# Hybrid gated-DeltaNet / mLSTM layer on one core: small-product banks kept by count, a decay chain on every second step, and a shorter last norm

## The chip, the cores and the metric

One Trainium2 chip, one of its cores. The metric is the device time of one execution in microseconds (us); lower is better. Three runs of the kernel before gave 1633.6, 1635.83 and 1637.04 us.

## The reference

One decoder layer, batch 1, 256 positions, width 2048, all in float32:

```python
shift, scale, gate = split(silu(c) @ w_ada + b_ada)
h = rms_norm(x, norm_pre_w) * (1 + scale) + shift
proj = h @ w_in                       # 12 segments, 24656 columns
o_a = gated_delta_rule(conv(q), conv(k), conv(v), decay, beta)    # 32 value heads, chunks of 64
y_a = (rms_norm(o_a) * silu(z)) @ w_proj_gdn
h_b = mlstm_chunkwise(conv(q), conv(k), v, i, f)                  # 8 heads
y_b = (sigmoid(o) * rms_norm(h_b) * silu(z)) @ w_proj_mlstm
out = (sigmoid(g_a) * y_a + sigmoid(g_b) * y_b) @ w_out
x + gate * rms_norm(out, norm_post_w)
```

The decay of the delta rule and the input and forget gates of the mLSTM come from 80 of the columns of `h @ w_in` (a softplus, exponentials and running sums along the sequence).

## The kernel before

The large products run on TensorE in a split form: each float32 weight tile `raw` is cast on ScalarE (ACT) to a reduced-precision `whi` (L168), the rest `wlo = raw - whi` is formed on VectorE (DVE) or, early on, GpSimd (POOL) (L169), and `mm3` (L217) sums three products. Four `whi` and four `wlo` buffers stand between these engines and TensorE, so a tile can be prepared up to four steps ahead.

The order of the work is fixed when the program is written, by two objects. `Stream` (L62) walks a list of weight units. Each unit has one or two uses, and one use is a **step**: 12 products of 512 columns or 24 products of 256 columns. After a use, the unit's `after` function may run, then `side.step()` is called once, then the next tile is prepared. `Side` (L30) holds generators of small work; a step lets each of them go on to its next `yield`. `wait(n)` yields n times. Each engine runs what it was given in that order, and never takes a later instruction first.

In order, the program goes through: the conditioning vector and the first gate columns (14 groups of 512 columns, added up over five blocks of rows by `add_start_groups`, L381); in the last block the 80 decay and gate columns come first (`add_ab`, product `pab`) and their chain `gates` (L433) runs as side work beside the 14 groups; then eight periods of delta-rule heads (`gdn_period`, L869), four rounds of mLSTM heads, the two output projections (`py`), and the last product `w_out` (`pw`).

In the last block of the 14 groups, every second step ends a group. Its `after` (L400) adds the two product banks to the sum so far on DVE (L405, twice), takes a sigmoid or silu of 1024 columns on ACT (L410), and stores it.

Within a period, side work prepares two head pairs (`gdn_stage1`, L604), inverts the chunk triangles (`base_inverse`, L670) and solves for the outputs (`gdn_stage2`, L725). The last of `gdn_stage2` transposes the outputs of two pairs into a bank each (`pt`, L848) and copies each bank out on ACT (`oT`, L850).

TensorE's result memory is used as four banks for the large products (`jtile`, pool `pj`) and four for the small ones (`gtile`, pool `pg`). The kernel keeps its own book of the small banks: `gtile` assumes that the four are given in turn, and `banks(n)` yields until the next n in turn were freed in an earlier step.

The last function, `finish` (L1168), closes the norm of one half of the rows: it sums four partial sums of squares, takes the power on POOL, and scales and adds the residual for four blocks of 512 columns, three on DVE (L1182) and one on ACT and POOL (L1179, L1180), each then stored.

Of the kernel before, what the change touches and what calls it, by code (L numbers as in the profile page):

```python
# [19 lines left out]
EPS = 1e-6  # L20
# [96 lines left out]
def hybrid_layer_kernel(  # L117
# [33 lines left out]
    pg = None  # L151
# [35 lines left out]
        split_w(raw[:, h * 1024:h * 1024 + n], hi[:, 0:n], lo[:, 0:n])  # L187
        return hi, lo

    freed = [-1] * 4  # L190
    slots = [0, {}]

    def gtile(nm, held=False):
        i = slots[0] % 4
        slots[0] += 1
        t = pg.tile([P, 512], F32, name=nm, tag="g")
        freed[i] = 1 << 30 if held else side.t + 1
        slots[1][id(t)] = i, t
        return t

    def gfree(t):
        freed[slots[1].pop(id(t))[0]] = side.t

    def banks(n):

        while any(freed[(slots[0] + j) % 4] >= side.t for j in range(n)):
            yield

    def jtile(nm):
        return pj.tile([P, 512], F32, name=nm, tag="pj")  # L210

    def pow_(o, i, e):
        G.tensor_tensor(o, i, e, op=ALU.pow)

    def mm3(ps, lhi, llo, rhi, rlo, start, stop):
        for i, (l, r) in enumerate(((lhi, rhi), (lhi, rlo), (llo, rhi))):
            T.matmul(ps, l, r, start=start and i == 0, stop=stop and i == 2, skip_group_check=True)  # L217

    side = Side()
    bp = x0 = y0 = None  # L220
# [52 lines left out]
    late_c = {}  # L273
# [64 lines left out]
    def ada_units():  # L338

        adders = []  # L340
        for k in range(KC):
            for pt in range(2):
                def prep(h, raw, k=k, pt=pt):
                    V.scalar_tensor_tensor(raw, raw, 1.0, csil, op0=ALU.mult, op1=ALU.mult,
                                           accum_out=ad[:, pt * KC + k:pt * KC + k + 1])
                    if 4 <= 2 * k + pt < 8:
                        j = 2 * (2 * k + pt)
                        if j > 8:
                            x_turn(j)
                        if j < 14:  # L350
                            x_scale(j + 2)
                    h_chunks(k - 1)
                    if pt == 1:
                        due.append(k)
                        if k == 0:
                            h_chunks(0)
                            x_chunks(6, 10)
                        elif k == KC - 1:
                            share[1] = 0.0
                    return ()  # L360
                adders.append(lambda i=2 * k + pt, prep=prep:
                              stream.add(w_ada[i], prep, None, 1, load=(load_ada, "ada", ADA_BUFS)))
        return adders

    br = ExitStack()

    def branches_open():

        nonlocal bp, pg, x0, y0
        side.drain()  # L370
        st.close()
        pcs.close()
        pg = ctx.enter_context(tc.tile_pool(name="pg", bufs=4, space=PSUM))
        bp = br.enter_context(tc.tile_pool(name="bp", bufs=2))

        x0 = bp.tile([P, 8, P], F32, name="x0", tag="x0", bufs=1)
        y0 = bp.tile([64, 8, 64], F32, name="y0", tag="y0", bufs=1)
        G.memset(x0, 0.0)
        G.memset(y0, 0.0)
# [53 lines left out]
    def gates(ps):  # L433
# [6 lines left out]
            return work[:, len(used) - 1]  # L440
        xb, ab, e, u, l, r = (t_(n) for n in ("xb", "ab", "e", "u", "l", "r"))
        V.tensor_scalar(xb, ps[:, 0:S], late_c["abb"][:, 0:1], None, op0=ALU.add)
        yield
        A.activation(ab, xb, AF.Abs)
        A.activation(e, ab, AF.Exp, scale=-1.0)
        na = gp.tile([32, 1], F32, name="na")
        A.activation(na, late_c["alog"], AF.Exp)
        yield
        V.tensor_scalar(u, e, 1.0, None, op0=ALU.add)
        yield  # L450
        A.activation(l, u, AF.Ln)
        A.activation(r, l, AF.Exp, scale=-1.0)
        yield
        V.tensor_scalar(u, u, -1.0, None, op0=ALU.add)
        V.tensor_tensor(e, e, u, op=ALU.subtract)
        V.tensor_tensor(e, e, r, op=ALU.mult)
# [13 lines left out]
                                 op0=ALU.mult, op1=ALU.add)  # L470
        V.tensor_tensor_scan(bf[96:104], on_[96:104], mn[96:104], 0.0, op0=ALU.mult, op1=ALU.add)
        SP.dma_start(bm[64:72], bf[96:104])
        yield
        A.activation(gt[32:64], mn[32:64], AF.Exp)
        yield
        V.tensor_tensor(gt[64:72], xb[64:72], bm[64:72], op=ALU.subtract)
        V.tensor_tensor_scan(mm_[64:72], zz[64:72], gt[64:72], 0.0, op0=ALU.add, op1=ALU.max)
        V.tensor_tensor(bm[64:72], bm[64:72], mm_[64:72], op=ALU.add)
        yield
# [4 lines left out]
        yield  # L484
        yield
        tp = jtile("tp")
        for b in range(2):
            T.transpose(tp[:, b * P:(b + 1) * P], gt[:, b * P:(b + 1) * P], ident)
            T.transpose(tp[:, S + b * P: S + (b + 1) * P], g2[:, b * P:(b + 1) * P], ident)
# [4 lines left out]
    def add_ab():  # L494
        st_ = {}

        def use(h, hi, lo):
            if h == 0:
                st_["ps"] = jtile("pab")
            for j in range(8):  # L500
                k = h * 8 + j
                h_chunks(k)
                mm3(st_["ps"][:, 0:S], hi[:, j * P:(j + 1) * P], lo[:, j * P:(j + 1) * P], h_hi[:, k], h_lo[:, k],
                    k == 0, k == KC - 1)
        stream.add(w_ab, prep_w, use, after=lambda: side.add(gates(st_["ps"])))
# [70 lines left out]
    o_dr = dr.tile([32, P, S], F32, name="o_dr")  # L576
    hb_dr = dr.tile([KC, P, S], F32, name="hb_dr")

    def wait(n):
        for _ in range(n):  # L580
            yield
# [22 lines left out]
    def gdn_stage1(p, ps, res):  # L604
# [48 lines left out]
        for blk, ps_, n, c0 in ((0, psa, 256, 0), (1, psb, 128, 512)):  # L653
            yield
            side.debt += 1.45 if blk == 0 else 1.0
            for h in range(2):
                V.scalar_tensor_tensor(au[:, h, c0:c0 + 2 * n].rearrange("p (a b) -> p a b", a=2),
                                       ps_[:, 0:2 * n].rearrange("p (a b) -> p a b", a=2), cj[:, blk, h:h + 1],
                                       dd[:, h, c0 // 2:c0 // 2 + n].unsqueeze(1).broadcast_to([P, 2, n]),
                                       op0=ALU.mult, op1=ALU.mult)  # L660
            gfree(ps_)
            if blk == 0:
                sk = bp.tile([P, 2], F32, name="sk", tag="sk")
                pow_(sk, sse[:, 2:4], phalf[:, 0:2])
# [60 lines left out]
    def gdn_stage2(zg, res, zr):  # L725
# [115 lines left out]
                                       op0=ALU.mult, op1=ALU.mult)  # L841
        yield from wait(2)
        yield from banks(2)
        for z in range(2):
            pt = gtile("pt", True)
            for h in range(2):
                for blk in range(2):
                    T.transpose(pt[:, h * S + blk * P:h * S + (blk + 1) * P], ons[z][:, blk, h], ident)  # L848
            oT = bp.tile([P, 2, S], F32, name="oT", tag="oT")
            A.activation(oT.rearrange("p h t -> p (h t)"), pt, AF.Copy, scale=late_c["gnw"][:, 0:1])  # L850
            gfree(pt)
            SP.dma_start(o_dr[4 * zg + 2 * z:4 * zg + 2 * z + 2].rearrange("h d t -> d h t"), oT)

    def period_tail(zg, ps, res, zr):
# [257 lines left out]
    def merge(hf, yb):  # L1112
# [26 lines left out]
        if hf == 1:  # L1139
# [17 lines left out]
    def out_part(b, ps, c0):  # L1157

        fp, mg = late["fp"], late["mg"]
        for i, p_ in enumerate(ps):  # L1160
            jk = fp.tile([P, 512], F32, name="fj", tag="fj", bufs=2)
            cg = c0 // 512 + i
            A.activation(jk, p_, AF.Square, accum_out=late["ssf"][:, b, cg:cg + 1])
        for i, p_ in enumerate(ps):
            cs = slice(c0 + i * 512, c0 + (i + 1) * 512)
            V.tensor_tensor(mg[:, b, cs], p_, late["bg"][:, cs], op=ALU.mult)

    def finish(b):  # L1168

        fp, ssf, mg, xr = (late[n] for n in ("fp", "ssf", "mg", "xr"))  # L1170
        sst = fp.tile([P, 1], F32, name=f"sst{b}")
        V.tensor_reduce(sst, ssf[:, b], axis=AX.X, op=ALU.add)
        V.tensor_scalar(sst, sst, 1.0 / D, EPS, op0=ALU.mult, op1=ALU.add)
        pow_(sst, sst, mhalf[:, 0:1])
        for cg in range(4):
            cs = slice(cg * 512, (cg + 1) * 512)
            yo = mg[:, b, cs]
            if cg == 3:
                A.activation(yo, yo, AF.Copy, scale=sst)  # L1179
                G.tensor_tensor(yo, yo, xr[:, b, cs], op=ALU.add)  # L1180
            else:
                V.scalar_tensor_tensor(yo, yo, sst, xr[:, b, cs], op0=ALU.mult, op1=ALU.add)  # L1182
            SP.dma_start(out[b * P:(b + 1) * P, cs], yo)

    def add_out_half():
# [13 lines left out]
    def add_out_group(g, held=0):  # L1199

        st_ = {"held": []}
        for t in range(4):
            def use(h, hi, lo, t=t):
# [15 lines left out]
                if k0 == KC - 2:  # L1219
                    for b in range(2):  # L1220
                        if b:
                            for a in st_["held"]:
                                block(1, *a)
                        out_part(b, st_["ps"][b:b + 1], 1024 + 512 * g)
                        if held:
                            finish(b)
            stream.add(w_o[8 + 4 * g + t], prep_w, use)

    for hf in range(2):
# [85 lines left out]
```

## Time and profile before

| | us |
|---|---|
| median of three runs | 1635.83 |
| the profiled execution | 1634.3 |
| its span (first to last instruction) | 1632.5 |
| TensorE busy within the span | 1595.8 |
| VectorE busy | 1137.3 |
| ScalarE busy | 937.5 |
| GpSimd busy | 241.7 |

The profiled execution lies 1.5 us below the median, and 1.8 us of it lie outside the span. Busy time of TensorE says that it had a product in work, not that it ran at its best rate; how fast it goes is read from the distance between the starts of two products.

### The profile page before, as it was taken

How to read it: one execution, taken by the hardware profiler on the slowest of the kernel's cores; microseconds unless marked ns; L12 is line 12 of the kernel's file. 1: busy time of each engine (PE TensorE's matmuls, PEld its weight loads, DVE VectorE, ACT ScalarE, POOL GpSimd, SP SyncE). 2: the span in 40 equal slices, each digit the busy share in tenths (PEclk: the TensorE clock that was granted, in tenths of full speed). 3: DMA queues.
4: the chain of work that ended last, by engine and by line, in shares of the span. 5: the costliest groups of instructions: out<-in, count | busy, mean ns of one | idle time of the engine just before them, and what ended most of it. 6: DMA issues, size and time to landing. Idle time of an engine off the chain costs nothing.

```text
span 1632.5 us, 25436 instructions
## 1 busy us (share of the span) xinstructions
PE 1595.8 (98%) x9844; PEld 1398.7 (86%) x9844; DVE 1137.3 (70%) x1793; ACT 937.5 (57%) x1496; POOL 241.7 (15%) x191
## 2 busy tenths in 40 slices
PE   6999999999999999999999999999999999999997
PEld 4888887799998999999898989889988788888886
DVE  5585556665678787969686969685878556756654
ACT  7744446665655575666666666665565544444443
POOL 3877760000000010000000000000100000100101
PEclk9999999999999999999999999999999999999999
DMA  9998775765454555454546464646888668766572
GB/s 370 387 364 321 280 272 180 259 245 187 166 197 165 183 175 185 165 184 160 185 161 197 162 198 152 193 167 247 299 301 310 236 235 301 275 233 252 194 278 103
DMA packets 96259, 372.37 MB, mean 228 GB/s; under 512 B 26261, under 2 KB 46213, under 8 KB 58249
## 3 DMA queue, kind: packets, MB, share of 16 engines
q1 hardware_dynamic: 96138, 370.75, 63.9%
q8 instruction: 77, 1.26, 0.3%
q14 instruction: 44, 0.36, 0.1%
HBM read 354.40 MB, written 16.31 MB: 227 GB/s over the span
## 4 chain that ended last, share of the span: by engine, by line
PE 78%; issue 13%; DVE 3%; ACT 2%; DMA 2%; POOL 1%; SPq 0%; DVEq 0%; POOLq 0%; ACTq 0%
PE pn L217 34%; PE pt L217 27%; PE py L217 8%; DVE wlo L169 1%; ACT whi L168 1%; POOL mg L1123 1%; PE psa L217 1%; DMA raw<-in_dram 1%; PE mq L766 1%; PE mz L774 1%; PE mp L741 1%; PE pt L848 0%; DMA ar<-in_dram 0%; PE po L811 0%; PE pc L801 0%
## 5 line engine op out<-in xcount | busy, mean ns | idle before, releaser
L169 DVE TENSOR_TENSOR wlo<-raw,whi 128x1024 fp32r<-128x1024 f32 x450 | 552.7, 1237 | 273.3 <-ACT whi L168 272.4
L168 ACT CAST whi<-raw 128x1024 fp32r<-128x1024 f32 x514 | 532.0, 1051 | 313.2 <-PE pn L217 145.7
L217 PE MATMUL pt<-h_hi,whi 128*128 128x256 f32 x1280 | 368.1, 288 | 0.0
L217 PE MATMUL pt<-h_hi,wlo 128*128 128x256 f32 x1280 | 362.6, 283 | 1.9 <-DVE wlo L169 1.9
L217 PE MATMUL pt<-h_lo,whi 128*128 128x256 f32 x1280 | 362.0, 283 | 0.0
L217 PE MATMUL pn<-whi,h_hi 128*128 128x512 f32 x896 | 354.3, 395 | 3.5 <-ACT whi L168 3.4
L217 PE MATMUL pn<-wlo,h_hi 128*128 128x512 f32 x896 | 350.5, 391 | 3.0 <-DVE wlo L169 3.0
L217 PE MATMUL pn<-whi,h_lo 128*128 128x512 f32 x896 | 350.4, 391 | 0.0
L217 PEld LDWEIGHTS pt<-h_hi,wlo 128*128 128x128 f32 x1280 | 245.1, 191 | 2.8 <-DVE wlo L169 2.7
L217 PEld LDWEIGHTS pt<-h_hi,whi 128*128 128x128 f32 x1280 | 245.2, 192 | 1.3
L217 PEld LDWEIGHTS pt<-h_lo,whi 128*128 128x128 f32 x1280 | 245.3, 192 | 0.2
L217 PEld LDWEIGHTS pn<-whi,h_hi 128*128 128x128 f32 x896 | 169.1, 189 | 40.1 <-ACT whi L168 3.8
L217 PEld LDWEIGHTS pn<-wlo,h_hi 128*128 128x128 f32 x896 | 169.2, 189 | 38.4 <-DVE wlo L169 4.3
L217 PEld LDWEIGHTS pn<-whi,h_lo 128*128 128x128 f32 x896 | 169.0, 189 | 35.8 <-POOL h_lo L169 0.3
L169 POOL TENSOR_TENSOR wlo<-raw,whi 128x1024 fp32r<-128x1024 f32 x64 | 153.6, 2408 | 44.2 <-ACT whi L168 44.2
L217 PE MATMUL py<-whi,yhi 128*128 128x512 f32 x384 | 150.6, 392 | 0.3 <-ACT vt L953 0.3
L217 PE MATMUL py<-whi,ylo 128*128 128x512 f32 x384 | 149.5, 389 | 0.0
L217 PE MATMUL py<-wlo,yhi 128*128 128x512 f32 x384 | 149.4, 389 | 0.0
L405 DVE TENSOR_TENSOR part<-pn,part 128x512 f32<-128x512 f32 x112 | 74.0, 687 | 48.0 <-PE pn L217 48.0
L168 ACT CAST yhi<-ya 128x512 fp32r<-128x512 f32 x48 | 29.9, 622 | 124.7 <-PE py L217 122.9
L169 DVE TENSOR_TENSOR ylo<-ya,yhi 128x512 fp32r<-128x512 f32 x48 | 33.2, 692 | 90.4 <-ACT yhi L168 88.4
L567 DVE SCALAR_TENSOR_TENSOR qs<-pt,gcv,qs 128x255 f32<-128x255 f32 (+2 forms) x192 | 92.2, 480 | 4.6
(243 smaller groups left out, 1800.5 us busy)
## 6 DMA issues: line engine op xcount, KB each, us to landing
raw<-in_dram SPq DMA_DIRECT2D x259, 1024.0 KB
ar<-in_dram SPq DMA_DIRECT2D x32, 1024.0 KB
raw<-in_dram SPq DMA_DIRECT2D x28, 512.0 KB
ya<-o_dr SPq DMA_DIRECT2D x32, 256.0 KB
gate_dr<-part SPq DMA_DIRECT2D x11, 512.0 KB
gb<-rows SPq DMA_DIRECT2D x20, 256.0 KB
ug<-ud SPq DMA_DIRECT2D x32, 128.0 KB
o_dr<-oT SPq DMA_DIRECT2D x16, 256.0 KB
```

The lines of the kernel that those rows point to most:

```text
L168: A.copy(hi, src)
L169: (eng or V).tensor_tensor(lo, src, hi.bitcast(F32), op=ALU.subtract)
L217: T.matmul(ps, l, r, start=start and i == 0, stop=stop and i == 2, skip_group_check=True)
L405: V.tensor_tensor(part[g][:, b], st_["ps"][b], part[g][:, b], op=ALU.add)
L567: V.scalar_tensor_tensor(dst[:, n, sh:], src[:, 0:S - sh], taps(n, 3 - sh), dst[:, n, sh:], op0=ALU.mult, op1=ALU.add)
L741: T.matmul(pss[t][o:o + 32, m * 32:(m + 1) * 32], um(m)[r:r + 32, o:o + 32], yc[r:r + 32, m], start=True, stop=True)
L766: T.matmul(psp[64:128, m * 64:(m + 1) * 64], um(m)[0:64, 64:128], y0[:, m], start=True, stop=True)
L774: T.matmul(psz[0:64, m * 64:(m + 1) * 64], p2[64:128, m], x0[64:128, m, 64:128], start=True, stop=True)
L1123: G.tensor_tensor(mcols(b, hf, cg), mcols(b, hf, cg), s_, op=ALU.add)
```

## The change

The book of small banks becomes a count: `taken` holds the tiles in use with the step from which each is free, and `banks(n)` goes on as soon as no more than 4 - n are in use, whichever they are. `gfree` can free a tile some steps late, which `gdn_stage1` uses for its first two. The four small banks are opened when the last conditioning unit has been prepared (`banks_open`), and not after the 14 groups, so that `pab` and the transpose `tp` of the decay chain live there and not among the large products' banks. In `gates`, each of nine `yield`s becomes `wait(2)`. In `gdn_stage2`, both `pt` banks are taken and all eight transposes are issued before the first copy. In the last norm, three of the four partial sums are added and scaled after the last group but one (`first_squares`); `finish` adds the fourth with one operation, weights the last block while the power runs, and does all four scale-and-add operations on DVE.

```diff
-    freed = [-1] * 4
-    slots = [0, {}]
+    taken = {}
     def gtile(nm, held=False):
-        i = slots[0] % 4
-        slots[0] += 1
         t = pg.tile([P, 512], F32, name=nm, tag="g")
-        freed[i] = 1 << 30 if held else side.t + 1
-        slots[1][id(t)] = i, t
+        taken[id(t)] = [t, 1 << 30 if held else side.t + 1]
         return t
-    def gfree(t):
-        freed[slots[1].pop(id(t))[0]] = side.t
+    def gfree(t, late=0):
+        taken[id(t)][1] = side.t + late
     def banks(n):
-        while any(freed[(slots[0] + j) % 4] >= side.t for j in range(n)):
+        while True:
+            for i in [i for i, q in taken.items() if q[1] < side.t]:
+                del taken[i]
+            if len(taken) + n <= 4:
+                return
             yield
...
                         elif k == KC - 1:
                             share[1] = 0.0
+                            banks_open()
...
+    def banks_open():
+        nonlocal pg
+        pcs.close()
+        pg = ctx.enter_context(tc.tile_pool(name="pg", bufs=4, space=PSUM))
...
         V.tensor_scalar(xb, ps[:, 0:S], late_c["abb"][:, 0:1], None, op0=ALU.add)
-        yield
+        yield from wait(2)
         A.activation(ab, xb, AF.Abs)
...
-        yield
-        yield
-        tp = jtile("tp")
+        yield from wait(2)
+        yield from wait(2)
+        tp = gtile("tp")
...
-                st_["ps"] = jtile("pab")
+                st_["ps"] = gtile("pab")
...
-            gfree(ps_)
+            gfree(ps_, 1)
...
+        pts = [gtile(f"pt{z}", True) for z in range(2)]
         for z in range(2):
-            pt = gtile("pt", True)
             for h in range(2):
                 for blk in range(2):
-                    T.transpose(pt[:, h * S + blk * P:h * S + (blk + 1) * P], ons[z][:, blk, h], ident)
+                    T.transpose(pts[z][:, h * S + blk * P:h * S + (blk + 1) * P], ons[z][:, blk, h], ident)
+        for z in range(2):
             oT = bp.tile([P, 2, S], F32, name="oT", tag="oT")
-            A.activation(oT.rearrange("p h t -> p (h t)"), pt, AF.Copy, scale=late_c["gnw"][:, 0:1])
-            gfree(pt)
+            A.activation(oT.rearrange("p h t -> p (h t)"), pts[z], AF.Copy, scale=late_c["gnw"][:, 0:1])
+            gfree(pts[z])
...
+    def first_squares():
+        late["ms"] = ms = late["fp"].tile([P, 2], F32, name="ms")
+        V.tensor_reduce(ms, late["ssf"][:, :, 0:3], axis=AX.X, op=ALU.add)
+        V.tensor_scalar(ms, ms, 1.0 / D, EPS, op0=ALU.mult, op1=ALU.add)
+    def finish(b, ps):
+        squares(b, [ps], 1536)
+        V.scalar_tensor_tensor(sst, ssf[:, b, 3:4], 1.0 / D, late["ms"][:, b:b + 1], op0=ALU.mult, op1=ALU.add)
         pow_(sst, sst, mhalf[:, 0:1])
+        row_weights(b, [ps], 1536)
         for cg in range(4):
             yo = mg[:, b, cs]
-            if cg == 3:
-                A.activation(yo, yo, AF.Copy, scale=sst)
-                G.tensor_tensor(yo, yo, xr[:, b, cs], op=ALU.add)
-            else:
-                V.scalar_tensor_tensor(yo, yo, sst, xr[:, b, cs], op0=ALU.mult, op1=ALU.add)
+            V.scalar_tensor_tensor(yo, yo, sst, xr[:, b, cs], op0=ALU.mult, op1=ALU.add)
             SP.dma_start(out[b * P:(b + 1) * P, cs], yo)
```

How the order moves, at three places. First ACT's queue in the last block of the 14 groups, at the second group of instructions of `gates` (a logarithm and an exponential, each behind a table load; in the rows `work` is the chain's tile, `part_105` and `part_106` are groups 1 and 2). Before:

```order
L168 CAST whi<-raw 128x1024
L451 ACT_TABLE_LOAD
L451 ACTIVATE work<-work 128x256
L452 ACT_TABLE_LOAD
L452 ACTIVATE work<-work 128x256
L168 CAST whi<-raw 128x1024
L410 ACT_TABLE_LOAD
L410 ACTIVATE part_105<-part_105 128x1024
```

and after:

```order
L168 CAST whi<-raw 128x1024 x2
L419 ACT_TABLE_LOAD
L419 ACTIVATE part_105<-part_105 128x1024
L168 CAST whi<-raw 128x1024 x2
L419 ACTIVATE part_106<-part_106 128x1024
L460 ACT_TABLE_LOAD
L460 ACTIVATE work<-work 128x256
L461 ACT_TABLE_LOAD
L461 ACTIVATE work<-work 128x256
L168 CAST whi<-raw 128x1024 x2
```

The chain's four instructions stood between the two casts of one group, in a step that ends no group; now they stand right behind a group's sigmoid, and both casts of the next group come after them.

Second, TensorE's queue at the output transposes of the fourth period (the semaphores that a row waits for are in brackets; `on` is the output, `pn` and `pt_7219` are large products). Before:

```order
L217 MATMUL pn_7545<-whi,h_lo 128x512
L848 MATMUL pt<-con,on 128x128 x4
L848 MATMUL pt<-con,on 128x128 [waits Activation_49]
L848 MATMUL pt<-con,on 128x128 x3
L217 MATMUL pn_7544<-whi,h_hi 128x512
```

and after:

```order
L217 MATMUL pt_7219<-h_hi,wlo 128x256
L853 MATMUL pt_7502<-con,on 128x128 [waits DVE_49,PE_49]
L853 MATMUL pt_7502<-con,on 128x128 [waits DVE_49] x3
L853 MATMUL pt_7503<-con,on 128x128 [waits DVE_49] x4
L217 MATMUL pn_7534<-whi,h_hi 128x512 [waits Activation_49]
```

The fifth transpose waited for ACT, and no longer does; the eight stand up to three steps earlier among the large products.

Third, DVE's queue at the very end, for the second half of the rows. Before:

```order
L1166 TENSOR_TENSOR mg<-pw_15453,bg 128x512
L1172 TENSOR_REDUCE sst_15585<-ssf 128x1
L1173 TENSOR_SCALAR sst_15585<-sst_15585 128x1
L1182 SCALAR_TENSOR_TENSOR mg<-mg,sst_15585,xr 128x512 x3
L1311 UNCONDITIONAL_BRANCH
```

and after:

```order
L1196 SCALAR_TENSOR_TENSOR mg<-mg,sst_15545,xr 128x512 x4
L1190 SCALAR_TENSOR_TENSOR sst_15583<-ssf,ms 128x1
L1172 TENSOR_TENSOR mg<-pw_15456,bg 128x512
L1196 SCALAR_TENSOR_TENSOR mg<-mg,sst_15583,xr 128x512 x4
L1328 UNCONDITIONAL_BRANCH
```

One small operation stands ahead of the power in place of the weighting and two small ones, and DVE has four of the closing operations in place of three.

## Rows read from the trace of the kernel before

**Rows 1.** The page, busy time of TensorE: busy us (share of span) xinstructions.

```profile
PE 1595.8 (98%) x9844; PEld 1398.7 (86%) x9844; DVE 1137.3 (70%) x1793; ACT 937.5 (57%) x1496; POOL 241.7 (15%) x191
```

**Rows 2.** Waits of TensorE: who waited for whom, us in total, times, longest.

```profile
PE pt L848 <- ACT oT L850: 3.9, 5, 0.8
PE tp L488 <- DVE part L405: 3.6, 1, 3.6
```

**Rows 3.** Windows, PE alone: stretch, us, PE busy (x), granted clock, DMA share, GB/s.

```profile
295.00:299.50 4.50, 4.50 (x16) 0.62 0.46 168
```

**Rows 4.** Timeline, PE, first products of the last block and after it: start, us, what.

```profile
264.46 0.40 PE L217 MATMUL pn<-whi,h_hi 128*128 128x512 f32 x1
...
348.50 0.28 PE L217 MATMUL pt<-h_hi,whi 128*128 128x256 f32 x1
```

**Rows 5.** Timeline, DVE, the adds of two groups late in that block.

```profile
305.48 1.28 DVE L405 TENSOR_TENSOR part<-pn,part 128x512 f32<-128x512 f32 x2
...
311.11 1.28 DVE L405 TENSOR_TENSOR part<-pn,part 128x512 f32<-128x512 f32 x2
```

**Rows 6.** Timeline, ACT and DVE, the chain `gates` and its neighbours in their queues.

```profile
265.50 0.41 ACT L444 ACTIVATE work<-work 128x256 f32<-128x256 f32 x1
...
267.64 1.03 ACT L168 CAST whi<-raw 128x1024 fp32r<-128x1024 f32 x1
...
273.18 1.28 ACT L451 ACT_TABLE_LOAD   x1
...
276.53 1.03 ACT L168 CAST whi<-raw 128x1024 fp32r<-128x1024 f32 x1
...
282.13 1.28 ACT L474 ACT_TABLE_LOAD   x1
...
283.87 1.04 ACT L168 CAST whi<-raw 128x1024 fp32r<-128x1024 f32 x1
...
279.93 0.28 DVE L454 TENSOR_SCALAR work<-work 128x256 f32<-128x256 f32 x1
...
284.33 2.36 DVE L169 TENSOR_TENSOR wlo<-raw,whi 128x1024 fp32r<-128x1024 f32 x2
```

**Rows 7.** Timeline, one `wlo` on DVE and the first product that reads it.

```profile
297.23 1.23 DVE L169 TENSOR_TENSOR wlo<-raw,whi 128x1024 fp32r<-128x1024 f32 x1 [2.06 <-ACT whi L168]
...
302.49 0.39 PE L217 MATMUL pn<-wlo,h_hi 128*128 128x512 f32 x1
```

**Rows 8.** Timeline, PE, a large product and the output transposes of one period.

```profile
690.71 0.39 PE L217 MATMUL pn<-whi,h_lo 128*128 128x512 f32 x1
...
691.62 0.60 PE L848 MATMUL pt<-con,on 128*128 128x128 f32 x4
693.00 0.66 PE L848 MATMUL pt<-con,on 128*128 128x128 f32 x4 [0.78 <-ACT oT L850]
693.41 0.48 PE L217 MATMUL pn<-whi,h_hi 128*128 128x512 f32 x1
```

**Rows 9.** Timeline, all engines, the end, from the last sum of squares on.

```profile
1623.55 0.19 ACT L1163 ACTIVATION_READ_ACCUMULATOR fj<-pw 128x1 f32 x1
1624.80 0.56 POOL L213 TENSOR_TENSOR sst<-sst,mhalf 128x1 f32<-128x1 f32 x1 [2.27 <-DVE sst L1173]
1625.39 1.42 DVE L1182 SCALAR_TENSOR_TENSOR mg<-mg,sst,xr 128x512 f32<-128x512 f32 x2 [0.67 <-POOL sst L213]
1626.19 1.74 POOL L1180 TENSOR_TENSOR mg<-mg,xr 128x512 f32<-128x512 f32 x1 [0.83 <-ACT mg L1179]
1626.72 1.75 DVE L1182 SCALAR_TENSOR_TENSOR mg<-mg,sst,xr 128x512 f32<-128x512 f32 x1
1628.93 0.38 SPq L1183 DMA_DIRECT2D out_dram<-mg  x1
```

**Rows 10.** The first period: a wait on ACT's timeline, and PE's waits in 475 to 520.

```profile
477.89 0.40 ACT L600 ACTIVATE dd<-dd,ngt 128x128 f32<-128x128 f32 x1 [5.14 <-POOL dd L592]
...
PE pt L217 <- DVE wlo L169: 1.9, 4, 1.1
```

More of the change, by code (lines that the diff above doesn't have):

```diff
@@ L217, in mm3, with wait @@
             T.matmul(ps, l, r, start=start and i == 0, stop=stop and i == 2, skip_group_check=True)
+    def wait(n):
+        for _ in range(n):
+            yield
     side = Side()
@@ L365, in hybrid_layer_kernel @@
     br = ExitStack()
+    def banks_open():
+        nonlocal pg
+        pcs.close()
+        pg = ctx.enter_context(tc.tile_pool(name="pg", bufs=4, space=PSUM))
     def branches_open():
-        nonlocal bp, pg, x0, y0
+        nonlocal bp, x0, y0
         side.drain()
         st.close()
-        pcs.close()
-        pg = ctx.enter_context(tc.tile_pool(name="pg", bufs=4, space=PSUM))
         bp = br.enter_context(tc.tile_pool(name="bp", bufs=2))
@@ L447, in gates @@
         A.activation(na, late_c["alog"], AF.Exp)
-        yield
+        yield from wait(2)
         V.tensor_scalar(u, e, 1.0, None, op0=ALU.add)
-        yield
+        yield from wait(2)
         A.activation(l, u, AF.Ln)
         A.activation(r, l, AF.Exp, scale=-1.0)
-        yield
+        yield from wait(2)
         V.tensor_scalar(u, u, -1.0, None, op0=ALU.add)
@@ L472, in gates @@
         SP.dma_start(bm[64:72], bf[96:104])
-        yield
+        yield from wait(2)
         A.activation(gt[32:64], mn[32:64], AF.Exp)
-        yield
+        yield from wait(2)
         V.tensor_tensor(gt[64:72], xb[64:72], bm[64:72], op=ALU.subtract)
@@ L478, in gates @@
         V.tensor_tensor(bm[64:72], bm[64:72], mm_[64:72], op=ALU.add)
-        yield
+        yield from wait(2)
         A.activation(g2[64:72], bm[64:72], AF.Exp, scale=-1.0)
@@ L483, in gates @@
         SP.dma_start(rows[32:40], mm_[64:72])
-        yield
-        yield
-        tp = jtile("tp")
+        yield from wait(2)
+        yield from wait(2)
+        tp = gtile("tp")
         for b in range(2):
@@ L577, in hybrid_layer_kernel @@
     hb_dr = dr.tile([KC, P, S], F32, name="hb_dr")
-    def wait(n):
-        for _ in range(n):
-            yield
     def decay_rows(row0):
@@ L1155, in merge, with squares, row_weights, out_part @@
                 SP.dma_start(xr[:, b], x[b * P:(b + 1) * P])
-    def out_part(b, ps, c0):
-        fp, mg = late["fp"], late["mg"]
+    def squares(b, ps, c0):
         for i, p_ in enumerate(ps):
-            jk = fp.tile([P, 512], F32, name="fj", tag="fj", bufs=2)
+            jk = late["fp"].tile([P, 512], F32, name="fj", tag="fj", bufs=2)
             cg = c0 // 512 + i
             A.activation(jk, p_, AF.Square, accum_out=late["ssf"][:, b, cg:cg + 1])
+    def row_weights(b, ps, c0):
         for i, p_ in enumerate(ps):
             cs = slice(c0 + i * 512, c0 + (i + 1) * 512)
[L1166 to L1173, printed above, removed]
+            V.tensor_tensor(late["mg"][:, b, cs], p_, late["bg"][:, cs], op=ALU.mult)
+    def out_part(b, ps, c0):
+        squares(b, ps, c0)
+        row_weights(b, ps, c0)
+    def first_squares():
[3 more added lines that the diff above has]
+    def finish(b, ps):
+        ssf, mg, xr = (late[n] for n in ("ssf", "mg", "xr"))
+        sst = late["fp"].tile([P, 1], F32, name=f"sst{b}")
+        squares(b, [ps], 1536)
+        V.scalar_tensor_tensor(sst, ssf[:, b, 3:4], 1.0 / D, late["ms"][:, b:b + 1], op0=ALU.mult, op1=ALU.add)
         pow_(sst, sst, mhalf[:, 0:1])
+        row_weights(b, [ps], 1536)
         for cg in range(4):
@@ L1223, in use @@
                                 block(1, *a)
-                        out_part(b, st_["ps"][b:b + 1], 1024 + 512 * g)
                         if held:
-                            finish(b)
+                            finish(b, st_["ps"][b])
+                        else:
+                            out_part(b, st_["ps"][b:b + 1], 1024 + 512 * g)
+                    if not held:
+                        first_squares()
             stream.add(w_o[8 + 4 * g + t], prep_w, use)
```

## The prediction

> **What bounds the kernel now.** I read the page's busy line first. TensorE is busy for 1595.8 us, 98% of the span, DVE for 70% and ACT for 57% [rows 1]. So a product that only moves costs what it cost before, and time can come from three places alone: moments in which TensorE stands still, stretches at a lower clock, and the end, after its last product. Second, its waits: five times a `pt` transpose waits for ACT, 3.9 us in all, and once `tp` waits 3.6 us for DVE [rows 2]. Third, the granted clock: it is 0.62 of 2.4 GHz between 295.0 and 299.5, mostly the lower level of 1.2 GHz, right behind the stop at `tp` [rows 3]; (1 - 0.62) x 4.5 = 1.7 us went there. Fourth, the timeline around these places. The profiled execution took 1634.3 us; the median of the runs, 1635.83, is 1.5 above it. I make the sum on 1634.3 and add 1.5.
>
> The unit for stalls is a step's length. Four large products lie between the starts 690.71 and 691.62, 0.2275 each [rows 8], so twelve take 2.73 and a pair of steps (one group of the last block) 5.46. The last block runs from 264.46 to 348.50, 84.0 us [rows 4], for 28 steps that would take 76.4. So **7.6 us** are lost there today: 3.6 at `tp`, 1.7 to the clock, the rest in shorter waits. That is the most that the chain's new places can give.
>
> **The chain every second step.** Each group closes a loop between two engines: DVE adds, ACT's sigmoid, ACT casts two `whi`, DVE forms two `wlo`, and only then come DVE's next adds. With nothing of the chain in it, the loop takes 311.11 - 305.48 = 5.63 us [rows 5], against TensorE's 5.46. It is the slower by 0.17, so what is put into it is never caught up before the block ends; it only eats the lead of the prepared tiles. That lead I take from a tile well after the chain: its `wlo` ends at 297.23 + 1.23 = 298.46 and is first read at 302.49, a lead of 4.0 [rows 7].
>
> Today some pieces of the chain stand in steps that end no group, beside TensorE's products, and the stop at `tp` gives the loop its lead back. With `wait(2)` every piece falls right behind a group's sigmoid, ahead of both casts of the next group, in the loop. What then waits behind it is the cast, behind that DVE's subtraction, behind that TensorE. The prices, from the first instruction of a piece to the next cast [rows 6]:
> - absolute value and exponentials, 265.50 to 267.64: 2.14
> - logarithm and exponential, each behind a table load, 273.18 to 276.53: 3.35
> - DVE's burst, 279.93 to 284.33: 4.40. Beside it ACT does its sigmoid and one cast (1.0 each) in any case, so I charge 4.40 - 2.03 = 2.37
> - one exponential behind its load, 282.13 to 283.87: 1.74, and a second of the same kind: 1.74
> - the copies out of `tp`, priced as the absolute value: 0.41
>
> That is 11.75; with a drift of 0.17 over 12 pairs, 2.0, it is 13.8. The lead takes off 4.0, and 9.8 would be lost instead of 7.6: **+2.2 us**. The stop at `tp` goes, since the transpose is issued in time for its bank among the small ones; `wlo` is late instead, from about the fourth group on. Lower clock behind such stops I charge at nothing, because then the loop, not TensorE, sets the pace. Bounds: -7.6 if nothing of this is lost, +6.2 if the lead gives nothing (13.8 - 7.6). I take +2.2, as the loop's own period is the nearest row.
>
> **Both `pt` banks at once.** In the row of one period, four transposes start at 691.62, the next four only at 693.00, after 0.78 of idle, and the next large product at 693.41 [rows 8]. The second four thus cost 0.41, the first four with the wait 1.38; without the wait both would cost 0.41. That is 0.97 in each of five periods [rows 2]: **-4.8 us**. In the new order the fifth transpose waits for DVE alone, as its neighbours do, and that result is several steps old. What could be late next is the second bank: `banks(2)` was called before too, so the two are free when it goes on. Bounds: -4.8 and 0.
>
> **The last norm.** Today the last sum of squares is read out by 1623.55 + 0.19 = 1623.74, the power runs from 1624.80 to 1625.36, the scale-and-add operations start 0.03 later, the third only ends at 1626.72 + 1.75 = 1628.47, and the last store is issued at 1628.93 [rows 9]. The first two start (1626.72 - 1625.39)/2 = 0.67 apart; the third takes 1.75 while POOL adds on its side. After the change one small operation follows the read-out (I take 0.2, as the read-out itself), then the power's 0.56, then four scale-and-adds: the first at about 1624.55, the last at 1626.55, ending 0.75 later (1.42 - 0.67) at 1627.3, its store right behind. Against 1628.93 that is **-1.5 us**, a little rounded down. The weighting of the last block now stands beside the power. If the power had to wait it out, one DVE operation of that size (1.42 / 2 = 0.71), the gain would be 0.8. The row shows that a DVE operation and one of POOL stretch each other when both read the memory of operands: 1.75 instead of 0.71. The Trainium skill ("SBUF — State Buffer", section "Who interferes with whom") says more closely that a DVE instruction with two SBUF inputs contends with a GpSimd instruction that reads SBUF, and one with at most one such input does not. The weighting reads one input from the result memory, so by that page the power is not held, and the whole -1.5 stands; the closing rows agree, since there both of DVE's inputs are in SBUF. Bounds: -1.5 and -0.8.
>
> **Edits at nothing.** The two small operations of `first_squares` run on DVE (70% busy) while TensorE still has a whole group's second half to do; uncovered they would cost some 0.4. Counting the banks lets small products go up to three steps earlier; their number stays, and TensorE does them whenever they come. The loads and stores that they bring on SP's queue move with them; that is the second rival. `pab` and `tp` in other banks cost nothing: those banks stand empty during the last block.
>
> **Sum:** +2.2 - 4.8 - 1.5 = -4.1, so 1630.2 for a profiled execution and **1631.7 us** for the median, 0.25% less. This kernel's measurement tells from no change about 0.2%, 3.3 us: faster means below 1632.6, slower above 1639.1.
>
> **The rivals.**
> *The chain costs nothing.* The stop, the clock and the late tiles all go, and no new wait comes: -7.6 - 4.8 - 1.5 = -13.9, 1621.9. For it speaks that ACT is idle 43% of the time; against it that the loop is already slower than TensorE with no chain in it [rows 5].
> *Slower: the first period's jam spreads.* There ACT waits 5.14 us for a mask of POOL, which needs the loaded `gb`, and TensorE then waits 1.9 us in four pieces for `wlo` [rows 10]. If small work that goes earlier brings `gb` and POOL's mask closer together in the later periods, the same costs at least 1.9 in each of five: 9.5 on top of the sum, 1641.2. It decides once ACT's wait for the mask passes the lead of about 4 us [rows 7]. Against it: those four pieces are the whole of what TensorE waits for `wlo` in all eight periods.
> *The change does not do what it says at `pt`.* If the fifth transpose still waits, for a bank or for ACT, the 4.8 stays and the sum is +0.7: 1636.5, no change.
>
> **How the numbers follow.** The sum as it stands gets 0.79, the chain at nothing 0.08, the spread jam 0.07, the wait that stays 0.06. Within the first case the centre lies only 0.9 below the limit of "faster", and the chain's term is uncertain by some 4 either way, so 0.45 of the 0.79 is faster, 0.32 the same, 0.02 slower. Together: faster 0.53, same 0.38, slower 0.09. The range: downwards, the chain without its drift and without the DVE burst (2.0 + 2.4 less) gives 1627.3; upwards, the chain without any lead (+4.0) gives 1635.7, and the third rival 1636.5, so I take 1627.3 to 1637.0. The other two rivals stay outside.
>
> **What would show it.** Right: no wait of `pt` for ACT; no wait of `tp`; in the last block, waits of products for `wlo` that grow from the fourth group on, and a block of about 86 us; closing operations 0.67 apart and a last store some 3.6 us after the read-out. Wrong: a last block of 80 us or less (the lead is larger than I read, or ACT catches up), waits of ACT for POOL's mask of several us in periods after the first, or a fifth `pt` transpose that still starts over 1 us after the first.

## The result and the profile after

The changed kernel takes 1641.14 us (median of 6 runs, 1639.1 to 1645.25) against 1635.68 for the kernel before: ratio 1.0038, interval 1.0024 to 1.0051. It is slower by 5.5 us, where 4.1 less was forecast, and lies above the range of 1627.3 to 1637.0. The profiled execution took 1639.1 us, 2.0 below its own median, and its span is 4.8 us longer than that of before. The page's busy line after, which answers to [rows 1], shows as good as the same work:

```profile
PE 1599.7 (98%) x9844; PEld 1400.0 (86%) x9844; DVE 1135.9 (69%) x1795; ACT 936.5 (57%) x1495; POOL 240.4 (15%) x189
```

Where the 4.8 us came from is read from four products that both programs have: the first of the last block of the 14 groups, the first behind it, the first `py` and the last `pw`. The timeline of TensorE in the kernel after (start, us, what):

```profile
264.61 0.40 PE L217 MATMUL pn<-whi,h_hi 128*128 128x512 f32 x1
...
351.38 0.28 PE L217 MATMUL pt<-h_hi,whi 128*128 128x256 f32 x1
...
1269.81 0.50 PE L217 MATMUL py<-whi,yhi 128*128 128x512 f32 x1
...
1629.19 0.39 PE L217 MATMUL pw<-whi,m_lo 128*128 128x512 f32 x1
```

The first two answer to [rows 4]; the last two stood at these times in the kernel before:

```profile
1263.17 0.50 PE L217 MATMUL py<-whi,yhi 128*128 128x512 f32 x1
...
1622.63 0.39 PE L217 MATMUL pw<-whi,m_lo 128*128 128x512 f32 x1
```

| stretch, us | before | after | change | forecast |
|---|---|---|---|---|
| last block of the 14 groups | 84.04 | 86.77 | +2.7 | +2.2 |
| from there to the first `py` (periods, mLSTM rounds) | 914.67 | 918.43 | +3.8 | -4.8 |
| from there to the last product | 359.46 | 359.38 | -0.1 | 0 |
| last product to the end of the span | 9.86 | 8.14 | -1.7 | -1.5 |

Two of the three terms came out as they were worked out. The third row holds the miss: 8.6 us between +3.8 and -4.8. TensorE's waits in the kernel after (who waited for whom, us in total, times, longest), in the block and then between 400 and 1100 us:

```profile
PE pn L217 <- DVE wlo L169: 3.8, 4, 2.1
PE pn L217 <- ACT whi L168: 1.4, 2, 0.7
```

```profile
PE pa L790 <- ACT x L780: 3.2, 2, 2.4
PE pt L217 <- DVE wlo L169: 1.9, 4, 1.0
PE mx L757 <- ACT pcm L748: 1.7, 1, 1.7
PE psa L217 <- DVE ql L622: 1.3, 1, 1.3
PE pb L797 <- ACT ys L791: 1.0, 2, 0.8
```

Both waits of [rows 2] are gone, `tp`'s and the five of `pt`. In the periods `pa`, `mx` and `pb` now wait, 5.9 us together, which they never did before; each waits for a copy of ACT. What ACT was doing is on its timeline ahead of the longest of these, with the wait of `pa` on TensorE's as the last row (kernel after):

```profile
896.39 0.40 ACT L605 ACTIVATE dd<-dd,ngt 128x128 f32<-128x128 f32 x1 [5.08 <-POOL dd L597]
...
900.10 0.58 ACT L780 COPY x<-mz 64x512 f32<-64x512 f32 x1
...
900.73 0.94 PE L790 MATMUL pa<-rr,x 128*128 128x128 f32 x6 [2.44 <-ACT x L780]
```

The same three in the kernel before:

```profile
888.83 0.58 ACT L775 COPY x<-mz 64x512 f32<-64x512 f32 x1 [2.46 <-PE mz L774]
...
891.36 0.41 ACT L600 ACTIVATE dd<-dd,ngt 128x128 f32<-128x128 f32 x1 [0.65 <-POOL dd L592]
...
893.40 0.83 PE L785 MATMUL pa<-rr,x 128*128 128x128 f32 x6
```

Before, the copy that `pa` needs stood ahead of the exponentials of the mask and ACT waited 0.65 us for POOL. Now ACT waits 5.08 us, and the copy stands behind that wait. For `pa` and `pb` this is what the second rival described, with these two as what comes late in place of `wlo`; `mx` turns out below to be another case. ACT's waits for the mask in the whole run, before and after (two kernels, one line each):

```profile
ACT dd L600 <- POOL dd L592: 21.9, 15, 5.1
```

```profile
ACT dd L605 <- POOL dd L597: 31.8, 12, 5.1
```

The totals hide where it matters. In the four passes whose masks end ACT's wait at 728, 811, 896 and 981 us (724, 807, 891 and 975 before), that wait was 0.3 to 0.7 us before, and is 3.2, 3.4, 5.1 and 2.6 now. The four waits of `pa` and `pb` stand right behind these four, one behind each.

### The profile page after: what moved, and what is told of

It reads as the page before. It is cut to its first block, busy times and chain, and to the rows that moved or that the text cites. A ratio compares the mean times of both kernels' runs of the same rounds, so it can differ in the third digit from the quotient of the medians.

```text
span 1637.3 us, 25438 instructions
## 1 busy us (share of the span) xinstructions
PE 1599.7 (98%) x9844; PEld 1400.0 (86%) x9844; DVE 1135.9 (69%) x1795; ACT 936.5 (57%) x1495; POOL 240.4 (15%) x189
## 4 chain that ended last, share of the span: by engine, by line
PE 75%; DVE 8%; ACT 7%; DMA 6%; issue 3%; SPq 1%; POOL 1%; POOLq 0%; DVEq 0%; ACTq 0%
PE pn L217 26%; PE pt L217 22%; PE py L217 16%; PE pw L217 5%; DVE wlo L169 3%; DMA gb<-rows 2%; ACT whi L168 2%; DMA raw<-in_dram 2%; DVE qs L576 1%; DVE part L414 1%; DVE au L662 1%; DMA ud<-au 0%; DMA o_dr<-oT 0%; PE pb L797 0%; DMA ar<-in_dram 0%
```

## The experiments

Each ratio is against the kernel before, run on the same chip (medians there 1635.4 to 1636.1), with its 95% interval. Theory 1, from the traces above: the count of banks lets the small products come where their operands aren't ready, and TensorE stands still for them. Theory 2, its rival: the double `pt` banks or the later chain shift what the small products meet, and the count is innocent.

### One part of the change at a time

**The count alone.**

```diff
-        while any(freed[(slots[0] + j) % 4] >= side.t for j in range(n)):
+        while True:
+            for i in [i for i, q in taken.items() if q[1] < side.t]:
+                del taken[i]
+            if len(taken) + n <= 4:
+                return
             yield
...
-            gfree(ps_)
+            gfree(ps_, 1)
```

> The kernel before with the count of banks alone (and the two banks freed a step late). Theory 1: waits at pa, pb, mx, mz of about 7 us appear; with the pt wait of 4.8 still there, 1641 to 1643. Theory 2: no such waits, 1635 to 1636.

1640.92 us, 1.0037 (1.0024 to 1.0050). TensorE's waits between 400 and 1100 us show the new ones, and `pt`'s gone though its code is the old:

```profile
PE pa L785 <- ACT x L775: 3.3, 2, 2.6
PE mx L752 <- ACT pcm L743: 1.8, 1, 1.8
PE pb L792 <- ACT ys L786: 1.7, 2, 1.4
```

So the count brings the loss, and it also brings the gain at `pt`.

**Both `pt` banks at once alone.**

```diff
+        pts = [gtile(f"pt{z}", True) for z in range(2)]
         for z in range(2):
-            pt = gtile("pt", True)
...
+        for z in range(2):
             oT = bp.tile([P, 2, S], F32, name="oT", tag="oT")
```

> The kernel before with both pt banks taken and all eight transposes issued before the first copy, nothing else. By the prediction's term and theory 1: no wait of pt for ACT, 4.8 less, 1631. Theory 2: waits elsewhere eat it up, 1634 to 1637.

1636.19 us, 1.0006 (0.9997 to 1.0014): nothing gained. The wait stands as in [rows 2]:

```profile
PE pt L848 <- ACT oT L851: 3.9, 5, 0.8
```

In the built program the two tiles of a pair have the same one of the eight banks in five of the eight periods, in this kernel as in the one before. The code asks for both ahead of the first copy, but transposes into the same bank wait until that copy is done, 0.78 us as in [rows 8]. With the count the two differ in all eight periods. My term was right in size, and put down to the wrong edit.

**The chain every second step alone**, with the banks that it needs.

```diff
                             share[1] = 0.0
+                            banks_open()
...
-        yield
+        yield from wait(2)
...
-        tp = jtile("tp")
+        tp = gtile("tp")
...
-                st_["ps"] = jtile("pab")
+                st_["ps"] = gtile("pab")
```

> The kernel before with the small banks opened early, pab and tp in them, and wait(2) in the chain, nothing else. By the prediction's term: the stop at tp is replaced by waits for wlo, 2.2 more, 1638 (the profile after shows 2.7 more up to the end of the block). Rival (the chain is harmless by itself): 1628 to 1635.

1639.59 us, 1.0027 (1.0018 to 1.0036): 4.2 more, where 2.2 to 2.7 was expected. The block took 86.8 us, as in the kernel after, which is 2.7 more than in the kernel before. Part of the rest shows in a wait that this kernel has too, though its book is the old one:

```profile
PE mx L757 <- ACT pcm L748: 1.0, 1, 1.0
```

**The small banks for `pab` and `tp` alone**: the diff above without its second piece, the chain's yields as before.

> The kernel before with the small banks opened early and pab and tp in them, the chain's yields untouched. If the stop at tp came from sharing a bank with the large products, it goes, and the block is about 2 us shorter (82.4 in the changed kernel with this spacing, 84.0 to 85.3 before): 1633.5. Rival (the stop is the chain's own, the transposed rows come late): 1635 to 1636.

1634.03 us, 0.9992 (0.9982 to 1.0001): the interval just reaches no change. The block lasts 346.12 - 263.72 = 82.4 us:

```profile
263.72 0.40 PE L217 MATMUL pn<-whi,h_hi 128*128 128x512 f32 x1
...
346.12 0.28 PE L217 MATMUL pt<-h_hi,whi 128*128 128x256 f32 x1
```

The stop at `tp` was the price of a bank shared with the large products; the wider spacing is not needed for it.

**The chain's spacing undone in the changed kernel**, at all nine places.

```diff
-        yield from wait(2)
+        yield
```

> The changed kernel with the chain at one yield per piece, as before, pab and tp staying in the small banks. By the prediction's term with the size that the profile after shows, 2.7 less: 1638.4. Rival (the chain's spacing costs nothing, the 2.7 come from the banks): 1641.

1637.05 us, 1.0007 (0.9997 to 1.0018), 4.1 below the changed kernel. The block is 82.4 us, 4.4 shorter. So measured against the same banks, the spacing costs some 4 us here; between the two runs above, with the old book, it is some 6 (1639.59 and 1634.03).

**The chain in the steps that end no group.**

```diff
         V.tensor_scalar(xb, ps[:, 0:S], late_c["abb"][:, 0:1], None, op0=ALU.add)
-        yield from wait(2)
+        yield from wait(1)
```

> The kernel before with small banks opened early, pab and tp in them, wait(2) between the pieces of the chain but one yield ahead of the first, so that the pieces fall in the steps that end no group, between the two casts of a group. Loop theory of the prediction (only a piece between a group's sigmoid and its casts costs time): neither the stop at tp nor the waits for wlo, block near 80 us in place of 84, 1630 to 1632. Rival (any chain spread over more steps costs as in the even steps, 1639.6): 1637 or more.

1640.61 us, 1.0040 (1.0024 to 1.0056): my loop theory fails here. The block takes 88.2 us, the longest of all. DVE's timeline and TensorE's long wait:

```profile
289.89 0.28 DVE L463 TENSOR_SCALAR work<-work 128x256 f32<-128x256 f32 x1
...
294.29 1.22 DVE L169 TENSOR_TENSOR wlo<-raw,whi 128x1024 fp32r<-128x1024 f32 x1
295.43 1.28 DVE L414 TENSOR_TENSOR part<-pn,part 128x512 f32<-128x512 f32 x2
```

```profile
296.26 0.47 PE L217 MATMUL pn<-whi,h_hi 128*128 128x512 f32 x1 [3.45 <-DVE part L414]
```

No product in the block waits for ACT's `whi` any more, but DVE's burst of 4.4 us now stands ahead of a group's adds, and TensorE waits 3.45 us for the bank that these adds set free. A place that is free for ACT's pieces isn't for DVE's.

**The last norm alone**, with `squares`, `row_weights`, `first_squares` and `finish` as in the change.

```diff
+                    if not held:
+                        first_squares()
...
-            if cg == 3:
-                A.activation(yo, yo, AF.Copy, scale=sst)
-                G.tensor_tensor(yo, yo, xr[:, b, cs], op=ALU.add)
-            else:
-                V.scalar_tensor_tensor(yo, yo, sst, xr[:, b, cs], op0=ALU.mult, op1=ALU.add)
+            V.scalar_tensor_tensor(yo, yo, sst, xr[:, b, cs], op0=ALU.mult, op1=ALU.add)
```

> The kernel before with the new closing of the last norm alone. By the prediction's term 1.5 less: 1634. Rival (power held up by the weighting, or the last operations stretched): 0 to 0.8 less, 1634.7 to 1635.5.

1634.01 us, 0.9988 (0.9979 to 0.9996): 1.7 less. The end of the kernel after shows each step as it was worked out:

```profile
1630.10 0.19 ACT L1167 ACTIVATION_READ_ACCUMULATOR fj<-pw 128x1 f32 x1
1630.33 0.16 DVE L1190 SCALAR_TENSOR_TENSOR sst<-ssf,ms 128x1 f32<-128x1 f32 x1 [1.87 <-ACT fj L1167]
1630.41 0.68 DVE L1172 TENSOR_TENSOR mg<-pw,bg 128x512 f32<-128x512 f32 x1
1630.57 0.56 POOL L213 TENSOR_TENSOR sst<-sst,mhalf 128x1 f32<-128x1 f32 x1 [4.88 <-DVE sst L1190]
1631.16 2.74 DVE L1196 SCALAR_TENSOR_TENSOR mg<-mg,sst,xr 128x512 f32<-128x512 f32 x4
...
1633.93 0.33 SPq L1197 DMA_DIRECT2D out_dram<-mg  x1
```

The power runs its 0.56 us beside the weighting and isn't held up, four scale-and-adds take 2.74 in place of three in 3.08, and the last store follows the read-out by 3.64 us (5.19 before). The Trainium skill ("SBUF — State Buffer", section "Who interferes with whom") has it that a DVE instruction with at most one SBUF input, outside the two-port modes, doesn't contend with GpSimd; this trace agrees, with the power's 0.56 us the same beside the weighting as alone.

### What makes the mask late

The mask (POOL, `dd`) needs the load of `gb`. DMA issues on SP's queue and POOL's first mask operation, kernel before:

```profile
878.85 2.04 SPq L163 DMA_DIRECT2D raw<-in_dram  x2
880.93 0.43 SPq L585 DMA_DIRECT2D gb<-rows  x1
...
890.91 0.77 POOL L592 TENSOR_SCALAR_AFFINE_SELECT dd<-gb 128x256 f32<-128x256 f32 x2 [33.27 <-DMA gb<-rows]
```

and after:

```profile
880.68 2.75 SPq L686 DMA_DIRECT2D ug<-ud  x4
883.48 0.92 SPq L163 DMA_DIRECT2D raw<-in_dram  x2
884.44 0.43 SPq L590 DMA_DIRECT2D gb<-rows  x1
...
895.95 0.76 POOL L597 TENSOR_SCALAR_AFFINE_SELECT dd<-gb 128x256 f32<-128x256 f32 x2 [34.55 <-DMA gb<-rows]
```

In both kernels `gb` is issued behind the four loads `ug` and two of `raw`, and the mask follows 10.0 us later before, 11.5 after (mostly 5.1 to 5.5 in the passes with `raw` alone close ahead of it). Its issue itself moved by 3.5 us, the mask by 5.0. But ACT was ready for the mask only 0.6 later, at 896.39 - 5.08 = 891.31 in place of 891.36 - 0.65 = 890.71, since the copy that had waited 2.46 us for `mz` no longer stood ahead. The whole kernel was 2.9 us behind shortly before (`psa` of the pair ahead starts at 852.32 in place of 849.43), so about half of the 4.4 us by which ACT's wait grew is a mask that comes later, and half is ACT coming to it sooner. The next run takes the late load away: `gb` is loaded where `gdn_stage1` begins.

```diff
     def gdn_stage1(p, ps, res):
...
+        gb = decay_rows(2 * p)
         yield from conv_silu(ps, lambda n, j: late_c["gcv"][:, (p * 4 + n) * 4 + j:(p * 4 + n) * 4 + j + 1], qs, qh,
                              0 if z else 3)
-        gb = decay_rows(2 * p)
         dd = decay_mask(gb)
```

**In the changed kernel:**

> The changed kernel with the load of gb issued at the start of gdn_stage1, some steps earlier on SP's queue, nothing else moved. Theory 1a (the count holds psa of the second pair a step longer, so the loads ud, ug and gb stand later on SP's queue, POOL's mask comes late, ACT waits up to 5 us for it, and the copies that pa, pb and mx need stand behind that wait): ACT's waits for the mask shrink to about 1 us and below, the 5.9 us of waits at pa, pb and mx go, time about 1635. Theory 1b (the small products simply stand too few steps behind their operands): the waits stay, about 1641.

1631.52 us, 0.9978 (0.9969 to 0.9986): 9.6 below the changed kernel, more than expected. ACT waits for the mask nowhere any more, `pa` and `pb` wait for nothing, and of the first period's waits only 1.0 us at `psa` is left:

```profile
PE mx L757 <- ACT pcm L748: 1.8, 1, 1.8
PE psa L217 <- DVE ql L622: 1.0, 1, 1.0
PE pt L217 <- ACT sz L871: 0.3, 1, 0.3
```

The wait of `mx` stays, so it isn't the mask's. ACT's queue shows what it hangs on. Kernel before, and this one:

```profile
1036.32 1.06 ACT L570 ACTIVATE mqk<-mqk 128x1024 f32<-128x1024 f32 x1 [2.08 <-DVE mqk L567]
...
1046.07 0.75 ACT L743 COPY pcm<-mp 32x256 f32<-32x256 f32 x2
```

```profile
1033.49 1.06 ACT L579 ACTIVATE mqk<-mqk 128x1024 f32<-128x1024 f32 x1 [3.30 <-DVE mqk L576]
...
1043.25 0.75 ACT L748 COPY pcm<-mp 32x256 f32<-32x256 f32 x2
```

From `mqk`, the activation of the first mLSTM round, to the copy that `mx` needs, ACT works without a gap for 9.75 us in both. `mqk` waits for DVE, and longer here, so the copy begins 5.4 us behind the product `mp` that it reads, in place of 3.4, and TensorE is at `mx` 4.0 us behind `mp`. Why DVE comes later to `mqk` stays open.

**In the kernel before:**

> The kernel before with the load of gb at the start of gdn_stage1 alone. If gb's load sets the mask in the kernel before too, ACT's wait of 5 us in the first period goes and TensorE's waits for wlo there (1.9) and at psa (1.3) with it: 1632.5. Rival (in the kernel before the mask is off the critical path, the jam of the first period is of another kind): 1635 to 1636.

1627.71 us, 0.9947 (0.9934 to 0.9959): 8.4 less, by one moved line. All that TensorE still waits for between 400 and 1100 us:

```profile
PE pt L848 <- DVE au L657: 0.5, 1, 0.5
```

With `gb` early the first period's waits go (1.9 us for `wlo` and 1.3 at `psa`), and those of `pt` too, 3.9: the two tiles now get different banks, as the built program shows. So about half of the gain is the mask's, and the other half came with the banks, which the moved line changed without being meant to.

**Which move of the count makes the load late.** The count lets `pt` go three steps earlier in three periods, where it takes banks that `psa` of the next pair had; and it lets `pb` follow `pa` by one step in place of two. First `pt` a step later, which puts `psa` back into its step in the later periods:

```diff
-        yield from wait(2)
+        yield from wait(3)
         yield from banks(2)
         pts = [gtile(f"pt{z}", True) for z in range(2)]
```

> The changed kernel with one more step before the pt banks are taken, so that psa of the second pair gets its three banks first and in the same step as in the kernel before (in the periods after the second), gb's load untouched. Theory 1a (pt, let three steps ahead by the count, takes the banks that psa had, and psa's step of delay makes ud, ug, gb and the mask late): ACT's waits for the mask return to 2 us and less, the waits at pa, pb and mx go, pt still doesn't wait for ACT: 1634 to 1636. Rival (the count itself, or the release a step late, makes the mask late): waits stay, 1640 or more.

1641.37 us, 1.0033 (1.0021 to 1.0044): theory 1a falls, `psa`'s step isn't enough; `pa`, `pb` and `mx` still wait 5.1 us. Then `pb`:

```diff
         gfree(pa)
-        yield
+        yield from wait(2 if 1 <= zg <= 5 else 1)
         yield from banks(1)
         pb = gtile("pb", True)
```

> The changed kernel with one step more before pb in the second to sixth of the eight solves, which alone puts psa, pa, pb, pc and po back into the steps of the kernel before (pt one step later than there), while the count, the double pt banks, the chain and the last norm stay as changed. Theory 1c (the step that the count saves at pb is what shifts the loads ud, ug and gb against the products, so ACT waits longer for the mask): ACT's wait before the mask's exponentials back to 2 to 3 us, no waits of 0.5 us or more at pa, pb and mx, pt without its waits, so before's time plus 2.7 to 4 (chain) less 4.8 (pt) less 1.7 (norm): 1631 to 1634. Rival 1d (the chain's or the double pt's timing makes the mask late whatever the steps): waits stay, 1639 to 1642.

1634.22 us, 0.9993 (0.9982 to 1.0003): 6.9 below the changed kernel. The waits of `pa` and `pb` are gone with the count still in place, and `pt` does not wait. The load is no faster here (10.0 to 11.9 us from the issue of `gb` to the mask in the four passes named under the result), and ACT still waits 0.6 to 2.5 us for the mask there, but no product stands still for it. Of TensorE's waits from 600 to 1100 us one is left, where none was expected:

```profile
PE mx L757 <- ACT pcm L748: 1.1, 1, 1.1
```

So what is lost at `pa` and `pb` hangs on the step that the count saved at `pb`. That step shifts `pc`, `po` and `pt` as well, and by them the banks of the next stage; with it given back, every small product of the periods but `pt` stands in its old step. The run shows that these moved steps are the cause; which of them makes `ug` and `gb` late wasn't taken apart.

### What the parts are worth with the load early

**The changed kernel with `gb` early and the chain's old spacing:**

> The changed kernel with the chain at one yield per piece (tp and pab in the small banks) and the load of gb early: both costs that the runs found taken away, the rest of the change kept. If the two are separate terms, 4.1 less than with gb early alone: 1627.4, the fastest so far. Rival (the block's time comes back later, since the loads set the pace): 1630 to 1632.

1625.16 us, 0.9941 (0.9924 to 0.9958): 6.4 below the run with `gb` early alone, where 4.1 was expected. So the spacing costs between 4 and 7 us, by what surrounds it.

**The kernel before with `gb` early, `pab` and `tp` in the small banks and the new last norm**, book in turn and old `pt` code:

> The kernel before with gb's load early, pab and tp in the small banks, and the new last norm: the book in turn and the old pt code kept. If the count of banks and the double pt are worth nothing once gb is early (both books then show no wait of pt for ACT), it is level with the changed kernel with early gb and the old chain, 1625.2, by the sum 1636.1 - 8.4 - 2.1 - 1.7 = 1623.9. Rival (the count is worth its 4.8 us at pt even then): 1629 to 1630.

1623.99 us, 0.9927 (0.9913 to 0.9941), the fastest of all and 11.4 below the kernel before; the sum had said 1623.9. The two intervals overlap: once `gb` is early, the count and the double `pt` are worth nothing that can be measured. Neither run has a wait of `pt` for ACT.

The changed kernel with the old book has no time: ordered that way, its instructions would wait for each other without end.

## Why the prediction was wrong

**The step that failed** is under "Edits at nothing": "Counting the banks lets small products go up to three steps earlier; their number stays, and TensorE does them whenever they come." TensorE takes them when they come, and then stands still until their operands do. The book in turn had made `pb` wait a step in five of the eight solves; with that step gone ACT comes to the exponentials of the mask sooner and the mask later, and waits that were harmless at 0.3 to 0.7 us became 2.6 to 5.1, with the copies for `pa` and `pb` behind them. The count alone costs 5.5 us net of what it gains at `pt`.

**The rival** that names this was in the list, with a time, 1641.2, that the median of 1641.14 meets; I gave it 0.07. That the two agree to 0.1 us is luck: its 9.5 was five times the first period's wait for `wlo`, and what came was 5.2 at `pa` and `pb`, 3.4 at `mx` that isn't the mask's, and half a us more at the chain. Its condition ("once ACT's wait for the mask passes the lead of about 4 us") didn't decide either, since TensorE stood still behind waits of 3.2 and 3.4. My ground against it was that TensorE waited for `wlo` in the first period only. That was the wrong row to ask: what counts is how far the mask is from being waited for, and ACT waited for it 15 times in the kernel before, 21.9 us in all. In the later periods it was late every time and cost nothing; its slack was used up. The place of `gb` in SP's queue stood in my working among the loads and stores that "move with" the products, and I didn't price it in the sum.

**The chain:** +2.2 forecast, +2.7 in the profile. The stop at `tp` went and waits for `wlo` and `whi` took its place, 5.2 us in six pieces, from the point that was named. Profiles of the same code of before gave 84.0 to 85.3 us for this block, so the size is not better known than by a us. What differs is the granted clock over the block: 0.98 where it took 84.0 and 84.1, 0.96 where it took 85.1 to 85.3. With the chain's pieces in the loop the clock made no difference, 86.8 us at 0.98 (the kernel after) and at 1.00 (the chain alone), as the working had it that charged the clock at nothing. But the kernel before was the wrong measure: with the small banks alone the block needs 82.4, and the spacing then costs 4.4 in it. And the loop as I drew it left out one edge, from DVE's adds back to TensorE's banks, which the chain in the odd steps ran into.

**The `pt` term:** -4.8 was the right size and it came. But "What could be late next is the second bank: `banks(2)` was called before too, so the two are free when it goes on" was wrong: the old book doesn't know which bank a tile gets, and in five periods the second tile got the bank of the first. The edit to which I credited the gain does nothing alone.

**The last norm:** -1.5 forecast, -1.7 in the profile and in the run of that part alone.

By the profile, then: +2.7 and -1.7 stand, and in place of -4.8 in the periods there is -4.8 and about 8.6 more. Of these 8.6, 5.9 are the five waits. Behind that of `mx` the granted clock is 0.87 of 2.4 GHz over 13 us, mostly at the upper of its two levels, for another 13 x 0.13 = 1.7; about 1.0 is left for the restarts. The starts of the same large products in both kernels split it the same way: 5.2 come at the four waits of `pa` and `pb`, 3.4 at that of `mx`. The window on TensorE (stretch, us, busy, granted clock, DMA share, GB/s):

```profile
1047.00:1060.00 13.00, 11.27 (x95) 0.87 0.60 168
```

## What to carry to other kernels

Before small work is let go earlier, look for engines that already wait for something at each pass without cost: there the slack is used up, and a step saved elsewhere turns that wait into a stall of the bound engine. Follow such a wait back to the instruction that issues its data; here a load that depends on nothing recent stood behind loads that do, and moving its issue alone took 8.4 us off, about half of them at the waits that it was meant for. The other half came because two tiles got other banks, so look at the banks too before an edit is given the credit. And when a wait goes after several edits, run each alone.

## What was not expected of the hardware

In the delta-rule passes of the kernels before and after, the 256 KB load `gb` took 5.1 to 6.3 us from issue to its first reader, and 7.7 to 11.5 us where four loads `ug` of 128 KB each had been issued a few us before on the same queue; a load of 1024 KB stood 0.4 or 0.5 us ahead of it in both cases. That `ug` makes the difference wasn't tested alone. And 0.97 us was lost five times per run at `pt` where both tiles had the same bank, and none where they had different ones, with the code of `pt` the same.
